# Scan of a Mamba-2 layer: the state's output moves into the chunk's own PSUM accumulation, with C times the decay made on VectorE

## The chip, the cores and the metric

The kernel runs on one core of one Trainium2 chip. The metric is the device time of one execution in microseconds, the median of several runs. All data are float32; large projections are made of three products of rounded halves (a high and a low part in fp32r), the scan's own products are plain float32.

## The reference, cut to what matters

The model is a trunk of two layers over 1024 positions of width 1024: a Mamba-2 layer, then shared keys and values, a stick-breaking attention layer, and a final norm. The change touches the Mamba-2 scan alone. Its step over chunks of 128 positions, for 4 groups of 8 heads (head width 64, state width 128):

```python
def step(state, inp):
    xc, ac, bc, cc = inp
    acum = jnp.cumsum(ac, axis=1)
    seg = jnp.where(causal, acum[:, :, None] - acum[:, None, :], -jnp.inf)
    scores = jnp.einsum('btgn,bsgn->btsg', cc, bc)[..., None] * jnp.exp(seg)
    y_diag = jnp.einsum('btsgh,bsghp->btghp', scores, xc)
    y_off = jnp.einsum('btgn,bghpn->btghp', cc, state) * jnp.exp(acum)[..., None]
    w_end = jnp.exp(acum[:, -1:] - acum)
    new_state = (state * jnp.exp(acum[:, -1])[..., None, None]
                 + jnp.einsum('bsgn,bsghp->bghpn', bc, xc * w_end[..., None]))
    return new_state, y_diag + y_off
```

After the scan come `y + d_skip * x`, the gate `y * silu(z)`, an RMS norm over each group's 512 channels, and the output projection. What the change rewrites is `y_diag + y_off`: exp(acum) may be multiplied onto C times the state, or onto C before the product.

## The kernel before, in words

**Stages.** First come the conditioning, the input projection and the causal convolution (to about 315 us of the span), then the scan (about 315 to 650 us), then the rest of the output projection, the shared keys and values, the attention and the final norm. The scan's inputs wait in DRAM: `xs_d` (convolved x, B, C), `ac_d` (acum per head), `ea_d` (exp(acum) per head).

**Units and chunks.** The scan works through 8 units: the 4 groups over the first half of the sequence, then the 4 groups over the second half. A unit has 4 chunks of 128 positions; the chunk index `c` runs from 0 to 7 in a group, and at c = 0 the state is empty. "The fourth unit" below is the last group over the first half (`st_2315` is its state); the fifth follows it.

**Names of one chunk.** `lm` (128x8x128) is acum broadcast to all partitions by a DMA (L509), masked on GpSimd (L515), passed through 8 exponentials on ScalarE (L518), and multiplied by `pb`, the scores C·B, on VectorE (L539). `xd` is x times dt (VectorE, from the transposes in `px`). `yd` (L550) is the chunk's own product, 8 matmuls of 64 output rows, one for each head; two heads lie side by side in one 128-row tile. `yo` (L560) is the state times C, 4 matmuls of 128 rows. `eb` is exp(acum) broadcast by two DMAs (L514), one for each half of the partitions, in a single buffer; VectorE multiplies `yo` by it (L562) and adds `yd` (L573), which gives `y`. `ps` (L565) is the new state's contribution `bs`·`xw`, added to the decayed state `sd` (GpSimd, L555) into `st`; at c = 0 ScalarE copies `ps` to `st` instead (L567), and VectorE copies `yd` to `y` (L571).

**What else TensorE does there.** Between these it projects z for the next unit: 3 k-steps of `pz` (a k-step is three matmuls, L129 to L131, with weights `hz`, `lz` split from the load `rz`), then the transposes of the next chunk, 3 more k-steps, the chunk's own products, 2 more k-steps. Before the products of a unit's third chunk stands `rs` (L599), the norm's sum of squares of the unit before: `gate` has made `y` times silu(z) (GpSimd), four squares on ScalarE (L587, L590) and their sums on GpSimd (L591). The last unit has no z left to project; there matmuls of the output projection (`po`, weights `ho`, `lo`, inputs `yh`, `yl`) stand between the chunks. Those inputs are the stored, normed y, loaded again (`yr`, L662, three buffers) and split on ScalarE (`yh`, L663) and VectorE (`yl`, L664) during the scan.

**What sets the order.** TensorE's order in the scan is that of the code. The order on VectorE, ScalarE, GpSimd and on SyncE, whose one queue issues all these loads, is set by a scheduler. Each engine works through its list in order, so an instruction that waits holds up what is listed behind it.

Of the kernel before, what the change touches and what calls it, by code (L numbers as in the profile page):

```python
# [12 lines left out]
F32 = mybir.dt.float32  # L13
# [39 lines left out]
def tile_trunk(ctx, tc, xT, xN, c, vec, ada0, adar, wxbc, wwave, wdt, wz, wmo, wk, wv, wq, wqz, wso, out):  # L53
# [413 lines left out]
    with ExitStack() as es:  # L467
# [32 lines left out]
        def chunk_a(u, c):  # L500
# [9 lines left out]
                        .rearrange("p (h t) -> p h t", t=P))  # L510
            eb = pq.tile([P, 4, P], F32, tag="eb", name="eb" + n, bufs=1)
            ev = ea_d[r0:r0 + 8, :].rearrange("(j a) t -> a j t", a=2)
            for a in range(2):
                Y.dma_start(out=eb[64 * a:64 * a + 64], in_=ev[a].partition_broadcast(64))  # L514
            Q.affine_select(out=lm, in_=lm, pattern=[[0, HPG], [1, P]], compare_op=ALU.is_ge,  # L515
                            fill=-1e30, base=0, channel_multiplier=-1)
            for h in range(HPG):
                e = S.activation(lm[:, h, :], lm[:, h, :], AF.Exp, bias=nac[:, c, h0_ + h:h0_ + h + 1])  # L518
                if g == 0 and c < 3:
                    tc.keep_in_program_order(e)  # L520
            px = ppt.tile([P, 512], F32, tag="px", name="px" + n)
            for j in range(4):
# [9 lines left out]
            if c < NC_ - 1:  # L532
                xw = py.tile([P, HPG, 64], F32, tag="xw", name="xw" + n)
                V.tensor_tensor(out=xw, in0=px3, op=ALU.mult,
                                in1=wdv[:, c, hsl].unsqueeze(2).to_broadcast([P, HPG, 64]))
                sp["xw"] = xw.rearrange("p h k -> p (h k)")
                sp["bs"] = py.tile([P, P], F32, tag="bs", name="bs" + n)
                S.copy(sp["bs"], pb[:, 0:P])
            V.tensor_tensor(out=lm, in0=pb[:, P:2 * P].unsqueeze(1).to_broadcast(sh3), in1=lm, op=ALU.mult)  # L539
            return sp, xd, lm, eb  # L540

        def chunk_b(u, c, sp, xd, lm, eb):
            g = u["g"]
            n = f"{g}_{c}"
            hsl = slice(HPG * g, HPG * g + HPG)
            cs = slice((c % CPH) * P, (c % CPH + 1) * P)
            ysl = u["y"][:, :, cs]
            yd = ppt.tile([P, 4, P], F32, tag="yd", name="yd" + n)
            for h in range(HPG):
                E.matmul(yd[64 * (h % 2):64 * (h % 2) + 64, h // 2, :], xd[:, h, :], lm[:, h, :],  # L550
                         start=True, stop=True)
            if 0 < c < NC_ - 1:

                sd = py.tile([P, HPG, 64], F32, tag="sd", name="sd" + n, bufs=1)
                Q.tensor_tensor(out=sd, in0=st[g].rearrange("p (h k) -> p h k", k=64), op=ALU.mult,  # L555
                                in1=eev[:, c, hsl].unsqueeze(2).to_broadcast([P, HPG, 64]))
            if c > 0:
                yo = ppt.tile([P, 4, P], F32, tag="yo", name="yo" + n)
                for j in range(4):
                    E.matmul(yo[:, j, :], st[g][:, j * P:(j + 1) * P], u["ct"][:, cs], start=True,  # L560
                             stop=True)
                V.tensor_tensor(out=eb, in0=yo, in1=eb, op=ALU.mult)  # L562
            if c < NC_ - 1:
                ps = ppt.tile([P, 512], F32, tag="ps", name="ps" + n)
                E.matmul(ps, sp["bs"], sp["xw"], start=True, stop=True)  # L565
                if c == 0:
                    S.copy(st[g], ps)  # L567
                else:
                    V.tensor_tensor(out=st[g], in0=ps, in1=sd.rearrange("p h k -> p (h k)"), op=ALU.add)
            if c == 0:  # L570
                V.tensor_copy(ysl, yd)  # L571
            else:
                V.tensor_tensor(out=ysl, in0=yd, in1=eb, op=ALU.add)  # L573

# [537 lines left out]
```

## Time and profile before

| | us |
|---|---|
| median of 3 runs | 1459.53 |
| lowest, highest | 1458.59, 1461.04 |
| the profiled execution's own time | 1462.46 |
| its span | 1460.8 |
| TensorE busy in the span | 1430.3 |
| VectorE, ScalarE, GpSimd busy | 962.0, 736.2, 516.5 |

The profile is one execution. A window row gives each engine's busy time in a stretch, TensorE's granted clock (1.00 is full speed) and the mean busy share of the 16 DMA engines. A timeline row gives start and length in us, and in brackets the idle time just before it with what ended it. The program counts a float32 matmul twice in the timeline (x16 for 8 matmuls). Where a `L` number stands, it is the line of the kernel.

### The profile page before, as it was taken

What the parts mean: (1) busy time and instruction counts of PE and PEld (TensorE: products, weight loads), DVE (VectorE), ACT (ScalarE), POOL (GpSimd) and SP (SyncE); (2) the same over time, 40 slices, a digit from 0 to 9 for tenths busy, and PEclk for the clock granted to TensorE, in tenths of its full rate; (3) what the DMA queues carried; (4) which work ended last, traced back from release to release, by engine and by line L of the source; (5) the groups of instructions that cost most, each with busy time, mean ns of one, the idle gap of its engine ahead of it and who ended that gap; (6) DMA issues with size and microseconds to landing.
All of it is one profiled execution on the core that took longest, in us unless ns stands there. A gap on an engine that the chain in (4) does not pass through costs nothing.

```text
span 1460.8 us, 20961 instructions
## 1 busy us (share of the span) xinstructions
PE 1430.3 (98%) x7772; PEld 1125.7 (77%) x7772; DVE 962.0 (66%) x1211; ACT 736.2 (50%) x1236; POOL 516.5 (35%) x601
## 2 busy tenths in 40 slices
PE   7998999999999999999999999999999999999997
PEld 4777888887777777778888888887777777777797
DVE  5699975455788887975733627516666666667674
ACT  6654533246666666733532424335555555556452
POOL 0021220002555555531011000027666666667531
PEclk9999999999999999999999999999999999999999
DMA  9358875233577766667433546460222122212253
GB/s 368 129 202 318 295 285 182 101 107 132 183 236 220 234 217 217 195 201 266 151 123 128 182 144 227 159 211 31 80 69 70 59 73 63 68 58 81 92 183 116
DMA packets 105446, 235.76 MB, mean 161 GB/s; under 512 B 9344, under 2 KB 40832, under 8 KB 103296
## 3 DMA queue, kind: packets, MB, share of 16 engines
q1 hardware_dynamic: 105344, 234.42, 47.8%
q8 instruction: 61, 1.00, 0.3%
q14 instruction: 41, 0.34, 0.1%
HBM read 188.51 MB, written 45.88 MB: 160 GB/s over the span
## 4 chain that ended last, share of the span: by engine, by line
PE 90%; DVE 5%; ACT 2%; issue 1%; DMA 1%; POOL 0%; SPq 0%; DVEq 0%; ACTq 0%; POOLq 0%
PE av L891 5%; PE pr L129 5%; PE pr L130 5%; PE pr L131 5%; PE sc L838 4%; PE at L870 4%; PE pz L129 4%; PE pz L131 4%; PE pz L130 4%; PE po L131 4%; PE po L130 4%; PE po L129 4%; PE pq L129 2%; PE pqz L129 2%; PE yd L550 2%; PE pq L131 2%
## 5 line engine op out<-in xcount | busy, mean ns | idle before, releaser
L861 POOL TENSOR_TENSOR be<-be,kp 128x1024 f32<-128x1024 f32 (+2 forms) x96 | 163.3, 1702 | 82.6 <-DVE kp L855 73.6
L841 ACT ACTIVATE kp<-sc 128x1024 f32<-128x1024 f32 (+2 forms) x96 | 75.5, 813 | 149.2 <-PE sc L838 111.3
L855 DVE TENSOR_TENSOR_SCAN kp<-kp,pone 128x128 f32<-128x128 f32 (+3 forms) x128 | 96.7, 803 | 63.8 <-POOL kp L848 63.8
L129 PE MATMUL pr<-h0h,hx 128*128 128x512 f32 x336 | 131.7, 392 | 3.8 <-DVE cv L353 3.8
L131 PE MATMUL pr<-h0h,lx 128*128 128x512 f32 x336 | 131.5, 391 | 0.0
L130 PE MATMUL pr<-h0l,hx 128*128 128x512 f32 x336 | 131.5, 391 | 0.0
L129 PE MATMUL pz<-h0h,hz 128*128 128x512 f32 x256 | 113.0, 441 | 0.0
L130 PE MATMUL po<-yl,ho 128*128 128x512 f32 x256 | 100.9, 394 | 0.6 <-DVE yl L664 0.6
L131 PE MATMUL po<-yh,lo 128*128 128x512 f32 x256 | 100.0, 391 | 1.3 <-DVE lo L124 1.3
L131 PE MATMUL pz<-h0h,lz 128*128 128x512 f32 x256 | 100.4, 392 | 0.0
L130 PE MATMUL pz<-h0l,hz 128*128 128x512 f32 x256 | 100.0, 391 | 0.0
L129 PE MATMUL po<-yh,ho 128*128 128x512 f32 x256 | 100.0, 391 | 0.0
L366 POOL TENSOR_TENSOR ar<-ar,crow 128x1024 f32<-128x1024 f32 x12 | 31.1, 2596 | 182.4 <-DMA ar<-adar 163.0
L518 ACT ACTIVATE lm<-lm,nac 128x128 f32<-128x128 f32 x256 | 78.9, 390 | 31.8 <-POOL lm L515 31.8
L855 DVE TENSOR_TENSOR_SCAN kp<-kp,ab,pone 128x512 f32<-128x512 f32 x64 | 78.3, 1265 | 24.7 <-ACT kp L841 14.2
L124 POOL TENSOR_TENSOR lq<-rq,hq 128x256 fp32r<-128x256 f32 x32 | 22.5, 738 | 177.8 <-ACT hq L123 177.8
L515 POOL TENSOR_SCALAR_AFFINE_SELECT lm<-lm 128x1024 f32<-128x1024 f32 x32 | 42.1, 1316 | 118.3 <-DMA lm<-ac_d 108.9
L555 POOL TENSOR_TENSOR sd<-st,eev 128x512 f32<-128x512 f32 x24 | 37.5, 1561 | 126.1 <-ACT st L567 114.2
L353 DVE SCALAR_TENSOR_TENSOR cv<-pr,vt,cv 128x1023 f32<-128x1023 f32 (+2 forms) x63 | 80.2, 1276 | 0.9
L129 PEld LDWEIGHTS pr<-h0h,hx 128*128 128x128 f32 x336 | 63.5, 189 | 17.4 <-issue 4.2
L123 ACT CAST ho<-ro 128x1024 fp32r<-128x1024 f32 x32 | 33.6, 1052 | 84.5 <-PE po L130 74.3
L870 PEld LDWEIGHTS at<-ident,be 128*128 128x128 f32 x576 | 67.2, 140 | 10.6 <-DVE aT L880 0.9
(258 smaller groups left out, 3886.7 us busy)
## 6 DMA issues: line engine op xcount, KB each, us to landing
ar<-adar SPq DMA_DIRECT2D x48, 512.0 KB, 5.3
lm<-ac_d SPq DMA_DIRECT2D x32, 512.0 KB, 5.0
rz<-wz SPq DMA_DIRECT2D x32, 512.0 KB, 3.8
ro<-wmo SPq DMA_DIRECT2D x32, 512.0 KB, 3.7
xs_d<-sv SPq DMA_DIRECT2D x24, 512.0 KB, 4.1
rx<-wxbc SPq DMA_DIRECT2D x21, 512.0 KB, 4.6
a<-ada SPq DMA_DIRECT2D x8, 1024.0 KB, 10.1
xg<-xs_d SPq DMA_DIRECT2D x8, 1024.0 KB, 6.1
```

Of the source, the lines that this page charges most:

```text
L129: E.matmul(ps, wh, xh, start=first, stop=False)
L130: E.matmul(ps, wh, xl, start=False, stop=False)
L131: E.matmul(ps, wl, xh, start=False, stop=last)
L353: V.scalar_tensor_tensor(out=ac[:, i:], in0=ps[:, :T - i], scalar=vv("cw", m * 4 + 3 - i), in1=ac[:, i:], op0=ALU.mult, op1=ALU.add)
L515: Q.affine_select(out=lm, in_=lm, pattern=[[0, HPG], [1, P]], compare_op=ALU.is_ge, fill=-1e30, base=0, channel_multiplier=-1)
L518: e = S.activation(lm[:, h, :], lm[:, h, :], AF.Exp, bias=nac[:, c, h0_ + h:h0_ + h + 1])
L838: E.matmul(ps[:, a, o:o + w], q[hsl[a], x, i * P:(i + 1) * P], kd[hsl[a], y, HT * c:HT * c + w], start=b == 0, stop=b == 2)
L841: S.activation(kp[:, :, ok:ok + w], ps[:, :, o:o + w], AF.Sigmoid, scale=-0.125)
L855: V.tensor_tensor_scan(out=ka, data0=ka, data1=pone.to_broadcast([P, w]), initial=1.0 if top else above[p, i][:, a, 0:1], op0=ALU.mult, op ...
L861: Q.tensor_tensor(out=be[:, :, o:o + w], in0=be[:, :, o:o + w], in1=kp[:, :, ok + 1:ok + w + 1], op=ALU.mult)
L870: E.transpose(ps[:, j, :], be[:, a, j * P:(j + 1) * P], ident)
L891: E.matmul(ps[hsl[a], cs], vd[:, j, hsl[a]], at[j // 4][:, a, j % 4, cs], start=j == 0, stop=j == nj - 1)
```

## The change

- `eb` becomes a tile of 128x8x128 with two buffers, the shape of `lm`: exp(acum) of 8 heads, broadcast to all 128 partitions by one DMA of 512 KB. It is loaded for c > 0 alone.
- VectorE multiplies it by C (`ct`), one instruction of 128x1024, both inputs in SBUF. It does not need the state, so it stands in `chunk_a`, a chunk ahead.
- TensorE: `yo` goes. For each pair of heads two matmuls of `xd`·`lm` start the accumulation in `yd`, and two of `st`·`eb` end it, all of 64 rows.
- ScalarE copies `yd` to `y` in every chunk; VectorE's product, addition and copy (L562, L573, L571) go.
- The PSUM bank of `yo` goes to `px`, which gets two. `xw` has one buffer instead of two. GpSimd's `sd` stands ahead of `yd` in the code.

```diff
-            eb = pq.tile([P, 4, P], F32, tag="eb", name="eb" + n, bufs=1)
-            ev = ea_d[r0:r0 + 8, :].rearrange("(j a) t -> a j t", a=2)
-            for a in range(2):
-                Y.dma_start(out=eb[64 * a:64 * a + 64], in_=ev[a].partition_broadcast(64))
+            eb = None
+            if c > 0:
+                eb = pq.tile(sh3, F32, tag="eb", name="eb" + n)
+                Y.dma_start(out=eb, in_=ea_d[r0:r0 + 8, :].rearrange("h t -> (h t)").partition_broadcast(P)
+                            .rearrange("p (h t) -> p h t", t=P))
...
-            px = ppt.tile([P, 512], F32, tag="px", name="px" + n)
+            px = ppt.tile([P, 512], F32, tag="px", name="px" + n, bufs=2)
...
-                xw = py.tile([P, HPG, 64], F32, tag="xw", name="xw" + n)
+                xw = py.tile([P, HPG, 64], F32, tag="xw", name="xw" + n, bufs=1)
...
             V.tensor_tensor(out=lm, in0=pb[:, P:2 * P].unsqueeze(1).to_broadcast(sh3), in1=lm, op=ALU.mult)
+            if c > 0:
+                V.tensor_tensor(out=eb, in0=ct[:, cs].unsqueeze(1).to_broadcast(sh3), in1=eb, op=ALU.mult)
...
-            yd = ppt.tile([P, 4, P], F32, tag="yd", name="yd" + n)
-            for h in range(HPG):
-                E.matmul(yd[64 * (h % 2):64 * (h % 2) + 64, h // 2, :], xd[:, h, :], lm[:, h, :],
-                         start=True, stop=True)
...
-            if c > 0:
-                yo = ppt.tile([P, 4, P], F32, tag="yo", name="yo" + n)
-                for j in range(4):
-                    E.matmul(yo[:, j, :], st[g][:, j * P:(j + 1) * P], u["ct"][:, cs], start=True,
-                             stop=True)
-                V.tensor_tensor(out=eb, in0=yo, in1=eb, op=ALU.mult)
+
+            yd = ppt.tile([P, 4, P], F32, tag="yd", name="yd" + n)
+            for j in range(4):
+                o = [yd[64 * a:64 * a + 64, j, :] for a in range(2)]
+                for a in range(2):
+                    E.matmul(o[a], xd[:, 2 * j + a, :], lm[:, 2 * j + a, :], start=True, stop=c == 0)
+                for a in range(2 if c > 0 else 0):
+                    h = 2 * j + a
+                    E.matmul(o[a], st[g][:, h * 64:h * 64 + 64], eb[:, h, :], start=False, stop=True)
...
-            if c == 0:
-                V.tensor_copy(ysl, yd)
-            else:
-                V.tensor_tensor(out=ysl, in0=yd, in1=eb, op=ALU.add)
+            S.copy(ysl, yd)
```

The scheduler's lists change with it, at three places that matter below. In a row of such a list a name's last number marks the instance, and "waits DMAHW2_49" names the queue or engine whose semaphore is waited for.

SyncE's queue in the fourth unit, before: the two loads of the unused `eb` of the fifth unit's chunk 0, then those of chunk 1 into the same buffer, then `lm`, the 1 MB load `xg` and the last `yr` of these.

```order
L662 DMA yr_0_5378<-ys_d_0_78 128x512 [waits DMAHW4_49,DMAHW2_49,DVE_49]
L514 DMA eb_0_3501<-ea_d 64x4x128 [waits DVE_49]
L514 DMA eb_0_3501<-ea_d 64x4x128 [waits DMAHW3_49]
L118 DMA rz_1_3_3857<-wz 128x1024 [waits DVE_49]
L514 DMA eb_1_3614<-ea_d 64x4x128 [waits DMAHW5_49,DMAHW3_49,DMAHW2_49]
L514 DMA eb_1_3614<-ea_d 64x4x128 [waits DMAHW6_49]
L509 DMA lm_3_3772<-ac_d 128x1024 [waits DMAHW7_49,PE_49]
L489 DMA xg_1_3588<-xs_d_70 128x4x512 [waits DMAHW0_49,DVE_49]
L662 DMA yr_0_5382<-ys_d_0_78 128x512 [waits DMAHW1_49,DVE_49]
```

The same stretch of SyncE's queue, now:

```order
L661 DMA yr_0_5410<-ys_d_0_76 128x512 [waits DMAHW7_49,DVE_49]
L509 DMA lm_2_3694<-ac_d 128x1024 [waits DMAHW0_49,PE_49]
L514 DMA eb_2_3696<-ea_d 128x1024 [waits DMAHW1_49,PE_49]
L661 DMA yr_0_5414<-ys_d_0_78 128x512 [waits DMAHW2_49,DVE_49]
L661 DMA yr_0_5418<-ys_d_0_78 128x512 [waits DMAHW3_49,DVE_49]
L489 DMA xg_1_3594<-xs_d_70 128x4x512 [waits DMAHW4_49,DVE_49]
L661 DMA yr_0_5422<-ys_d_0_78 128x512 [waits DMAHW7_49,DMAHW5_49,DVE_49]
L118 DMA rz_1_3_3867<-wz 128x1024 [waits DMAHW6_49,DVE_49]
L509 DMA lm_3_3780<-ac_d 128x1024 [waits PE_49]
```

No load of a chunk 0's `eb` stands there any more, `eb` waits for TensorE's last use of its buffer instead of VectorE's and a landing, and `yr` stands ahead of `xg`.

ScalarE at the start of the fifth unit, before: the state's copy first, the squares among the `yh` casts, the fourth square behind the last `yh` and 8 exponentials.

```order
L567 COPY st_2315<-ps_0_3661 128x512
L587 ACTIVATE sq_0_3569<-y_0_2847 128x512
L123 CAST hz_1_2_3758<-rz_1_2_3756 128x1024
L663 CAST yh_0_5332<-yr_0_5374 128x512
L590 ACTIVATE sq_0_1_3575<-y_0_2847 128x512
L590 ACTIVATE sq_0_2_3580<-y_0_2847 128x512
L663 CAST yh_0_5334<-yr_0_5378 128x512
L482 COPY sz_1_3594<-pz_1_0_3602 128x512
L538 COPY bs_2_3716<-pb_2_3709 128x128
L663 CAST yh_0_5336<-yr_0_5382 128x512
L518 ACTIVATE lm_3_3772<-lm_3_3772,nac 128x128 x8
L590 ACTIVATE sq_0_3_3585<-y_0_2847 128x512
```

The same place of ScalarE's list, now:

```order
L539 COPY bs_1_3645<-pb_1_3638 128x128
L586 ACTIVATE sq_0_3575<-y_0_2847 128x512
L589 ACTIVATE sq_0_1_3581<-y_0_2847 128x512
L589 ACTIVATE sq_0_2_3586<-y_0_2847 128x512
L572 COPY y_0_3224<-yd_0_3658 128x4x128
L569 COPY st_2315<-ps_0_3667 128x512
L662 CAST yh_0_5376<-yr_0_5418 128x512
L123 CAST hz_1_2_3766<-rz_1_2_3764 128x1024
L482 COPY sz_1_3600<-pz_1_0_3608 128x512
L589 ACTIVATE sq_0_3_3591<-y_0_2847 128x512
```

Three squares and the copy of `yd` stand ahead of the state's copy; the fourth square stands ahead of the exponentials and of all `yh` casts but one.

TensorE in the last unit, before: the products of chunk 6 in one piece, between matmuls of the output projection.

```order
L131 MATMUL po_0_5487<-yh_0_5336,lo_0_0_5491 128x512
L550 MATMUL yd_6_5229<-lm_6_5133,xd_6_5157 64x128 x8
L560 MATMUL yo_6_5240<-ct_1_4712,st_2315 128x128 x4
L565 MATMUL ps_6_5246<-xw_6_5159,bs_6_5161 128x512
L129 MATMUL po_0_5487<-yh_0_5338,ho_0_1_5520 128x512
```

The same chunk in TensorE's list, now:

```order
L130 MATMUL po_0_5465<-yl_0_5395,ho_0_1_5498 128x512
L561 MATMUL yd_6_5271<-lm_6_5171,xd_6_5194 64x128 x2
L131 MATMUL po_0_5465<-yh_0_5394,lo_0_1_5499 128x512
L129 MATMUL po_0_5465<-yh_0_5396,ho_0_1_5498 128x512
L130 MATMUL po_0_5465<-yl_0_5397,ho_0_1_5498 128x512
L131 MATMUL po_0_5465<-yh_0_5396,lo_0_1_5499 128x512
L130 MATMUL po_0_5531<-yl_0_5369,ho_0_0_5534 128x512
L131 MATMUL po_0_5531<-yh_0_5368,lo_0_0_5535 128x512
L129 MATMUL po_0_5531<-yh_0_5370,ho_0_0_5534 128x512
L130 MATMUL po_0_5531<-yl_0_5371,ho_0_0_5534 128x512
L564 MATMUL yd_6_5271<-eb_6_5173,st_2315 64x128 x2
L561 MATMUL yd_6_5271<-lm_6_5171,xd_6_5194 64x128 x2
```

The first two matmuls of 64 rows stand alone, eight of the output projection follow, and the other fourteen come after them; chunk 7 is split in the same way.

## Rows read from the trace of the kernel before

**Rows 1.** The page: span, and the chain that ended last, by engine.

```profile
span 1460.8 us, 20961 instructions
...
PE 90%; DVE 5%; ACT 2%; issue 1%; DMA 1%; POOL 0%; SPq 0%; DVEq 0%; ACTq 0%; POOLq 0%
```

**Rows 2.** Windows: PE, PEld, DVE, ACT, POOL busy (count), granted clock, DMA share, GB/s.

```profile
315.00:650.00 335.00, 330.03 (x1941) 258.16 (x1940) 270.93 (x320) 211.65 (x448) 151.47 (x104) 0.99 0.61 198
450.00:460.00 10.00, 9.62 (x57) 7.12 (x57) 10.00 (x11) 9.97 (x18) 8.89 (x6) 1.00 0.71 187
470.00:480.00 10.00, 8.01 (x39) 6.01 (x40) 6.17 (x9) 6.88 (x17) 4.42 (x4) 0.83 0.48 157
600.00:620.00 20.00, 18.18 (x98) 13.81 (x97) 20.00 (x22) 15.95 (x32) 12.80 (x9) 1.00 0.61 196
```

**Rows 3.** TensorE's waits in the scan: total us, times, longest.

```profile
PE rs L599 <- POOL sq L591: 2.8, 1, 2.8
PE po L131 <- DVE lo L124: 1.3, 1, 1.3
PE po L130 <- DVE yl L664: 0.6, 2, 0.3
```

**Rows 4.** TensorE's timeline, fifth unit: products of chunks 0 and 1.

```profile
451.07 1.09 PE L550 MATMUL yd<-lm,xd 128*64 128x128 f32 x16
...
452.66 0.80 PE L129 MATMUL pz<-h0h,hz 128*128 128x512 f32 x1
...
459.89 1.09 PE L550 MATMUL yd<-lm,xd 128*64 128x128 f32 x16 [0.38 <-DVE lm L539]
460.91 1.16 PE L560 MATMUL yo<-ct,st 128*128 128x128 f32 x8
461.91 1.02 PE L565 MATMUL ps<-xw,bs 128*128 128x512 f32 x2
462.37 0.80 PE L129 MATMUL pz<-h0h,hz 128*128 128x512 f32 x1
```

**Rows 5.** TensorE's timeline, fifth unit: the norm's sum and chunk 2.

```profile
471.99 1.12 PE L599 MATMUL rs<-sq,ones 128*128 128x512 f32 x2 [2.77 <-POOL sq L591]
473.05 1.97 PE L550 MATMUL yd<-lm,xd 128*64 128x128 f32 x16
474.95 1.89 PE L560 MATMUL yo<-ct,st 128*128 128x128 f32 x8
476.67 1.02 PE L565 MATMUL ps<-xw,bs 128*128 128x512 f32 x2
```

**Rows 6.** ScalarE's timeline in the fifth unit.

```profile
457.22 0.58 ACT L567 COPY st<-ps 128x512 f32<-128x512 f32 x1
...
467.04 0.62 ACT L663 CAST yh<-yr 128x512 fp32r<-128x512 f32 x1 [5.05 <-DMA yr<-ys_d]
467.57 2.45 ACT L518 ACTIVATE lm<-lm,nac 128x128 f32<-128x128 f32 x8
469.92 0.61 ACT L590 ACTIVATE sq<-y 128x512 f32<-128x512 f32 x1
```

**Rows 7.** SyncE's queue: its wait in 449 to 472 us, and an issue.

```profile
SPq L514 <- DMA eb<-ea_d: 3.8, 1, 3.8
...
458.64 0.32 SPq L662 DMA_DIRECT2D yr<-ys_d  x1
```

**Rows 8.** Landing of `yr` (425 to 475 us).

```profile
DMA to landing us min/median/max: 3.5/4.5/8.4
```

**Rows 9.** One instruction, ns min/median/max: `lm` and `lz` on VectorE.

```profile
L539 DVE TENSOR_TENSOR lm<-pb,lm x32: 1203/1211/1225, 329.8 to 627.1; 128x1024 f32<-128x1024 f32 x32
...
L124 DVE TENSOR_TENSOR lz<-rz,hz x31: 1208/1520/2304, 314.5 to 583.3; 128x1024 fp32r<-128x1024 f32 x31
```

**Rows 10.** Groups by form: busy us, mean ns | idle before, releaser.

```profile
L562 DVE TENSOR_TENSOR eb<-yo,eb 128x512 f32<-128x512 f32 x28 | 19.2, 684 | 7.9 <-PE yo L560 4.3 <-DMA eb<-ea_d 3.3
...
L573 DVE TENSOR_TENSOR y<-yd,eb 128x512 f32<-128x512 f32 x28 | 19.2, 684 | 0.4
...
L482 ACT COPY sz<-pz 128x512 f32<-128x512 f32 x32 | 18.5, 578 | 0.0
```

## The prediction

> **What bounds the kernel now.** I read first the chain that ended last: 90% of it is TensorE [rows 1]. Then the scan's window: TensorE is busy in 330.03 of 335.00 us, so at most 4.97 us of waiting can be won there, at a granted clock of 0.99; VectorE has 270.93, ScalarE 211.65, the DMA engines a share of 0.61 [rows 2]. Outside the scan the change touches only a few loads and products that fall into slack of the convolution. So the questions are: does TensorE's own work in the scan change, which of the four waits go, and which new one comes. The list of TensorE's waits names them: 2.8 us before the norm's sum `rs`, 1.3 and 0.6 before `po` in the last unit [rows 3], and 0.38 before `yd`, in the bracket of its row [rows 4]. Their sum, 5.1, is the window's idle time.
>
> The large wait has a tail. After it `yd` takes from 473.05 to 474.95, 1.90 us, where it took 1.02 (459.89 to 460.91) two chunks earlier, and `yo` 1.72 (474.95 to 476.67) instead of 1.00 [rows 4, 5]; the window 470 to 480 has a granted clock of 0.83 [rows 2]. TensorE had idled 2.77 us just before. The stretch ran at half clock, 1.2 instead of 2.4 GHz, and cost 0.88 + 0.72 = 1.60 us more.
>
> Where that wait comes from I followed backwards. `rs` waits for GpSimd's sum, that for ScalarE's fourth square, which started at 469.92, behind 8 exponentials (2.45 us), behind a `yh` cast at 467.04 that had waited 5.05 us for its load [rows 6]. The load `yr` was issued at 458.64 and landed 8.4 us later (the median is 4.5) [rows 7, 8]. It was late at SyncE: the queue stood 3.8 us, at the load of chunk 1's `eb`, until the unused `eb` of chunk 0 had landed in the same buffer [rows 7]; behind it came `lm`, the 1 MB `xg`, then `yr`.
>
> **The change part by part.**
>
> *TensorE.* A chunk with state lasts from `yd` at 459.89 to the next `pz` at 462.37, 2.48 us; one without state from 451.07 to 452.66, 1.59 [rows 4]. So the 8 records of `yo` cost 0.89, 0.11 each. The 16 of `yd` take 1.02; at half clock 1.90. With a part f that does not scale, 2 × (1.02 − f) + f = 1.90, so f = 0.14 and the matmuls are 0.88, 0.055 each: two of 64 rows take the time of one of 128, side by side. The 16 new records of `st`·`eb` in the same alternation cost 0.88 for 0.89 removed: −0.01 × 28 chunks = −0.3. Bounds: without overlap 16 × 0.11 = 1.78, +0.89 × 28 = +24.9; if f is a start-up that adjoining work hides, nothing below −0.3. I take −0.3, as the new matmuls have the shape, the width and the pairing of the row. In the last unit the list now splits chunks 6 and 7, two matmuls and then fourteen; that makes two more groups of 64 rows, each with an f of 0.14 in and, I assume, as much out: 2 × 0.28, about +0.5 (0 to +0.6).
>
> That f is the row's. The Trainium skill, "TensorEngine Tiling (Array Packing)", section "Key Properties", says that a change of the tiling mode drains the engine; it gives no price, so by it alone the split is a loss of unknown size, which the 0.14 of this trace agrees with.
>
> *VectorE.* Out go 28 products and 28 additions of 0.684 each, and 4 copies of about that [rows 10]: 41.0 us. In come 28 products of 128x1024 with two SBUF inputs. The trace has no such instruction; nearest are `lm`, same size with one input in PSUM, 1.21 us at any time, and `lz`, same size with both in SBUF, 1.21 to 2.30, median 1.52 [rows 9]. So 28 × (1.21 to 2.30) = 34 to 64; I take `lz`'s median, 42.6, since both inputs match. Net +1.6 of 270.9, ends −7 and +23. The 64 us left idle hide the mean case, but not in places: VectorE is busy 20.00 of 20.00 us between 600 and 620, in the last unit, and 10.00 of 10 between 450 and 460 [rows 2]. In return the product stands a chunk ahead and no longer between TensorE's product and `y`. `xw` in one buffer makes its product wait for `ps` of the chunk before; behind `lm` in VectorE's list it has most of a 9 us chunk to spare: nothing, or 0.4 if it delays the next product.
>
> *ScalarE.* In come 32 copies of 128x512 out of PSUM; the copy of `pz` takes 0.578 [rows 10]: +18.5 on 211.65, which TensorE's 330 us covers. It does not cover one place, the start of the fifth unit: 9.97 of 10 us busy [rows 2]. There the state's copy ended at 457.22 + 0.58 = 457.80 [rows 6], and TensorE reads it from chunk 1 on: before at `yo`, 460.91, now inside `yd`, which without its 0.38 wait starts at 459.51 [rows 4]. The margin was 3.1 and is 1.7. In front of that copy now stand two more copies of `yd` (1.16) and three squares (0.61 each, 1.83), 3.0 in all: 1.3 late. Against that, ScalarE's chain there starts with a `yh` cast that waits for a `yr` load; a load 1 us earlier gives 1 us back, one with the longest landing instead of the median takes 8.4 − 4.5 = 3.9 [rows 8]. I take a new wait of 1.0, near the row's own reckoning; bounds 0 and 3.9.
>
> *Loads.* 64 loads of 128 KB become 28 of 512 KB: 8.4 MB become 14.7, +6.3 on the 66 MB that 198 GB/s move in 335 us [rows 2]. The share goes from 0.61 to 0.67, not the bound; transfers may land later, which the 3.9 above holds. SyncE's 3.8 us stop goes: the load behind it is no longer made, and the new `eb` waits for TensorE's `yd` of chunks long done.
>
> *The old waits.* With `yr` ahead of `xg` and the fourth square ahead of the exponentials and the later casts, the sum for `rs` should be ready some 4 us earlier than 471.99, more than the 2.77: −2.77, and −1.60 for the clock. The 0.38 goes with the reordering of VectorE's list. The last unit's 1.3 + 0.6 I leave: they end with splits of weights and inputs that VectorE makes, and VectorE is full there. What is late next is the state's copy above.
>
> **Sum.** −2.77 − 1.60 − 0.38 = −4.75; +1.0 new wait; −0.3 + 0.5 on TensorE: −3.55. The profiled execution took 1462.46 (span 1460.8 [rows 1]) and would take 1458.9; it lies 2.9 above the median of 1459.53, so the forecast for the median is 1456.0. Its own range: the new wait from 0 to 2.5, the split from 0 to 0.6, and spread between runs: 1453.5 to 1458.6. A difference under 0.2%, 2.9 us, can't be told from none here.
>
> **Rivals.**
>
> *B, the wait comes back.* ScalarE at the start of the fifth unit becomes what the SyncE stop was. For it: 9.97 of 10 busy and 3.0 us put in front of a copy that TensorE needs. Against it: the chain can start earlier with its load. Price: a wait of 1.3 plus half of the 3.9 is 3.2, as long as the one that was followed by half clock, so +1.6 again: −4.75 + 3.2 + 1.6 + 0.2 = +0.25, 1459.8. No change.
>
> *C, all waits go.* If the new product a chunk ahead relieves VectorE in the last unit, 1.9 more goes and the new wait does not come: −4.75 − 1.9 − 0.3 + 0.5 = −6.45, 1453.1. Against it: VectorE's sum there does not fall.
>
> *D, slower: VectorE's product pays for two SBUF inputs.* `lz` reaches 2.30, `lm`, of the same size with one, never passes 1.23 [rows 9]; GpSimd works 8.89 of 10 and 12.80 of 20 us just in those windows [rows 2]. At 2.30 a product and sum of 1.37 is replaced by 0.93 more. Where VectorE is full TensorE sees it: three products in the last unit's full window, +2.8, and one at each of the six other gates, whose sums VectorE starts, +5.6. The waits that I strike then stay, because the squares come later: 1459.5 + 8.4 = 1467.9. It decides from a mean of about 1.8 us upward, where 9 × 0.43 uses up the 3.55. Against it: the median of `lz` is 1.52.
>
> The Trainium skill, "SBUF — State Buffer", section "Who interferes with whom", states that a VectorE instruction with two SBUF inputs contends with a GpSimd instruction that reads SBUF, and one with a single SBUF input does not. The trace agrees in that `lz` spreads from 1.21 to 2.30 us and `lm` does not. By this rule the product that is added is of the exposed kind and both that go are not, which is rival D.
>
> *E, the pairs do not overlap.* If matmuls that end an accumulation cannot run side by side as those that start it: +24.9, 1480.9. Against it: the pairing is that of the row; the trace has no accumulating pair.
>
> **How the numbers follow.** Forecast 0.42, B 0.30, C 0.10, D 0.13, E 0.05. Range: below, C's case less 2, 1451.0; above, half of D, 1464.0; E, the upper part of D and C's tail stay out, about 0.2. Faster by over 0.2% means under 1456.6: of the forecast 0.26, of B 0.03, C 0.10: 0.39. Slower means above 1462.4: D 0.13, E 0.05 and 0.04 of B: 0.22. Within: 0.16 + 0.23 = 0.39.
>
> **What would show it.** Right: no wait before `rs` in the fifth unit and a full granted clock in it; no SyncE wait at `eb`; a block of 2.4 to 2.5 us from `yd` to the next `pz`; copies of about 0.58 on ScalarE; `eb` products with a mean near 1.5. A wait of TensorE for ScalarE's copy of `ps` or `yd` at chunk 1 of the fifth unit shows the new term, with its size. Wrong: blocks of 3.3 us (E), products over 1.8 with VectorE ending TensorE's waits (D), or a wait in another unit where ScalarE or a load is late, which I have not priced.

## The result, and the profile after

The changed kernel is slower. Its first four executions gave 1476.84 us in the median (1473.34 to 1480.69) against 1459.06 for the kernel before, a ratio of 1.0123 [1.0086, 1.0160]; four more gave 1475.93 and 1.0114 [1.0101, 1.0127]. The forecast was 1456.0. The profiled execution took 1473.34 us. Of the first four executions two took 1473.3 and 1473.5 us, at a mean granted clock of 0.995, and two 1480.2 and 1480.7, at 0.992 and 0.990; what parts the pairs stays open.

The page after answers to [rows 1]: the chain that ended last is TensorE's to 81% instead of 90%; VectorE and the DMAs now hold 8% and 3% of it.

```profile
span 1471.6 us, 21305 instructions
...
PE 81%; DVE 8%; DMA 3%; ACT 2%; POOL 2%; issue 2%; SPq 0%; DVEq 0%; POOLq 0%; ACTq 0%
```

The scan's window, as the first row of [rows 2]: VectorE is no busier than before (267.67 for 270.93), ScalarE a little more. In a full stretch of 335 us TensorE idles 15.4 instead of 5.0.

```profile
315.00:650.00 335.00, 319.63 (x2110) 246.60 (x2109) 267.67 (x279) 223.03 (x473) 158.62 (x102) 0.99 0.63 214
```

TensorE's waits in the scan, as [rows 3]. Their sum is 15.3 us, 10.2 more than before; the two profiled executions differ by 10.9. So the loss is waiting. 9.0 us of it are put down to VectorE (2.3 before), 4.5 to ScalarE (none before) and 1.8 to GpSimd (2.8 before).

```profile
PE pz L131 <- DVE lz L124: 4.1, 6, 1.8
PE ps L567 <- DVE st L571: 3.6, 3, 1.6
PE yd L561 <- ACT st L569: 3.0, 1, 3.0
PE rs L598 <- POOL sq L590: 1.8, 1, 1.8
PE po L129 <- ACT yh L662: 1.5, 1, 1.5
PE po L130 <- DVE yl L663: 1.3, 1, 1.3
```

The `rs` of this list is in the last unit. In the fifth unit `rs` no longer waits, as forecast.

TensorE's own work is what was forecast. A chunk with state, as the second half of [rows 4]: each row is one input of a pair of heads, the rows start some 0.22 us apart, and from `yd` to the next `pz` it is 512.17 to 514.63, 2.46 us for 2.48 before.

```profile
512.17 0.44 PE L561 MATMUL yd<-lm,xd 128*64 128x128 f32 x4
512.44 0.39 PE L564 MATMUL yd<-eb,st 128*64 128x128 f32 x4
...
514.07 1.12 PE L567 MATMUL ps<-xw,bs 128*128 128x512 f32 x2
514.63 0.80 PE L129 MATMUL pz<-h0h,hz 128*128 128x512 f32 x1
```

The new instructions, grouped by form as [rows 10]: the product takes 1.44 us in the mean (1.52 was taken), the copy 0.574 (0.578). New is the idle time on the right: VectorE stood 25.9 us before the product, waiting for its load. Of VectorE's waits in 315 to 650 us the same wait is 21.4; for the `eb` of the kernel before it was 3.3 [rows 10].

```profile
L542 DVE TENSOR_TENSOR eb<-ct,eb 128x1024 f32<-128x1024 f32 x28 | 40.3, 1439 | 25.9 <-DMA eb<-ea_d 25.9
...
L572 ACT COPY y<-yd 128x512 f32<-128x512 f32 x32 | 18.4, 574 | 8.2 <-PE yd L564 8.1
```

Why the load is late shows in the landing times of the two kernels (loads, KB each, median us from issue to landing):

```profile
eb<-ea_d SPq DMA_DIRECT2D x64, 128.0 KB, 3.3
...
eb<-ea_d SPq DMA_DIRECT2D x28, 512.0 KB, 5.9
```

VectorE reads `eb` about as long after the issue as before: in the median 8.3 us now, and 7.7 from the later of the two loads before. But the load takes 5.9 us to land instead of 3.3, so that in the median 1.3 us are left between landing and use where 4.4 were; 13 of the 28 products start as their load lands. An estimate from the 11 waits in 315 to 650 us (0.6 to 3.5 us each): if each load had landed 2.6 us sooner, about 2 of the 21.4 us would be left. No run tried smaller loads.

How this reaches TensorE can be read in three places. First, VectorE's timeline in a later unit. At 540.36 it is done with `st` and waits 2.27 us for the decay's load; the split `lz` stands behind the product.

```profile
539.68 0.68 DVE L571 TENSOR_TENSOR st<-ps,sd 128x512 f32<-128x512 f32 x1
542.63 1.25 DVE L542 TENSOR_TENSOR eb<-ct,eb 128x1024 f32<-128x1024 f32 x1 [2.27 <-DMA eb<-ea_d]
543.80 2.10 DVE L124 TENSOR_TENSOR lz<-rz,hz 128x1024 fp32r<-128x1024 f32 x1
```

TensorE's timeline: it needed that `lz` 0.58 us earlier than it was there.

```profile
545.96 0.50 PE L131 MATMUL pz<-h0h,lz 128*128 128x512 f32 x1 [0.58 <-DVE lz L124]
```

SyncE's timeline: the next weight load `rz` goes out the moment `lz` has freed its buffer, and the next decay's load 0.9 us behind it. VectorE's next product starts at 553.07, after 3.09 us of waiting.

```profile
545.93 0.33 SPq L118 DMA_DIRECT2D rz<-wz  x1
546.32 0.42 SPq L509 DMA_DIRECT2D lm<-ac_d  x1
546.83 0.38 SPq L514 DMA_DIRECT2D eb<-ea_d  x1
```

Second, a unit's end in the first half. The gate's four sums (L582) can start as soon as ScalarE has copied `yd`, and stand in VectorE's list ahead of the state's sum `st`, which frees the bank of `ps`.

```profile
448.20 2.73 DVE L582 SCALAR_TENSOR_TENSOR y<-xg,vt,y 128x512 f32<-128x512 f32 x4
450.85 0.68 DVE L535 TENSOR_TENSOR xw<-px,wdv 128x512 f32<-128x512 f32 x1
451.45 0.67 DVE L571 TENSOR_TENSOR st<-ps,sd 128x512 f32<-128x512 f32 x1
```

TensorE's next `ps` waits for it, and ten microseconds later comes the third place, which the prediction had named: `yd` waits for the state's copy.

```profile
452.18 1.13 PE L567 MATMUL ps<-xw,bs 128*128 128x512 f32 x2 [1.55 <-DVE st L571]
...
462.59 0.44 PE L561 MATMUL yd<-lm,xd 128*64 128x128 f32 x4 [3.02 <-ACT st L569]
```

ScalarE's timeline there, as [rows 6]: a `yh` cast waited 7.42 us for its `yr`, and the whole list behind it came late, the state's copy to 462.02 from 457.22.

```profile
450.37 0.62 ACT L662 CAST yh<-yr 128x512 fp32r<-128x512 f32 x1 [7.42 <-DMA yr<-ys_d]
...
462.02 0.58 ACT L569 COPY st<-ps 128x512 f32<-128x512 f32 x1
```

### The profile page after: what moved, and what is told of

Same layout as the page of the kernel before. It is cut to its first block, busy times and chain, and to the rows that moved or that the text cites. A ratio compares the mean times of both kernels' runs of the same rounds, so it can differ in the third digit from the quotient of the medians.

```text
span 1471.6 us, 21305 instructions
## 1 busy us (share of the span) xinstructions
PE 1430.2 (97%) x7996; PEld 1122.6 (76%) x7996; DVE 964.0 (66%) x1179; ACT 752.1 (51%) x1268; POOL 529.7 (36%) x601
## 4 chain that ended last, share of the span: by engine, by line
PE 81%; DVE 8%; DMA 3%; ACT 2%; POOL 2%; issue 2%; SPq 0%; DVEq 0%; POOLq 0%; ACTq 0%
PE av L890 5%; PE pr L129 4%; PE pr L131 4%; PE pr L130 4%; PE sc L837 4%; PE at L869 4%; PE po L131 4%; PE po L129 4%; PE po L130 4%; PE pz L131 2%; PE pq L129 2%; PE pz L129 2%; PE pz L130 2%; PE pqz L129 2%; PE pq L131 2%
## 5 line engine op out<-in xcount | busy, mean ns | idle before, releaser
L554 POOL TENSOR_TENSOR sd<-st,eev 128x512 f32<-128x512 f32 x24 | 33.7, 1406 | 167.8 <-ACT st L569 118.3
L869 PEld LDWEIGHTS at<-ident,be 128*128 128x128 f32 x576 | 67.2, 140 | 10.4 <-DVE aT L879 0.7
L869 PE MATMUL at<-ident,be 128*128 128x128 f32 x576 | 74.7, 272 | 0.5 <-DVE aT L879 0.5
## 6 DMA issues: line engine op xcount, KB each, us to landing
a<-ada SPq DMA_DIRECT2D x8, 1024.0 KB, 10.2
```

Source lines behind the costliest of these rows:

```text
L869: E.transpose(ps[:, j, :], be[:, a, j * P:(j + 1) * P], ident)
```

## The experiments

All ratios are to the kernel before, on the same chip, with a 95% interval. "Product" is VectorE's C times decay, "load" that of the decay. The runs were made on several chips, on which the kernel before has medians of 1459.2 to 1460.2 us; differences between medians of different chips carry that much more.

| run | what | median us | ratio |
|---|---|---|---|
| e1 | changed kernel again | 1475.93 | 1.0114 [1.0101, 1.0127] |
| e2 | before, no unused load | 1458.60 | 0.9996 [0.9988, 1.0005] |
| e3 | no product | 1463.11 | 1.0025 [1.0015, 1.0035] |
| e4 | copies on VectorE | 1471.14 | 1.0085 [1.0065, 1.0105] |
| e5 | `st` ahead of the gate's sums | 1472.79 | 1.0093 [1.0077, 1.0108] |
| e6 | load on ScalarE's queue | 1476.70 | 1.0111 [1.0096, 1.0126] |
| e7 | product pinned late | 1636.21 | 1.1217 [1.1200, 1.1233] |
| e8 | product on GpSimd | 1480.88 | 1.0147 [1.0133, 1.0161] |
| e9 | before again, one execution | 1460.89 | |
| e10 | product, no load | 1466.41 | 1.0048 [1.0036, 1.0060] |
| e11 | no product, no load | 1462.14 | 1.0012 [1.0000, 1.0023] |
| e12 | C from PSUM | 1479.23 | 1.0135 [1.0122, 1.0149] |
| e13 | control: two `yr` buffers | 1484.83 | 1.0176 [1.0163, 1.0189] |
| e14 | e13, third decay buffer | 1478.74 | 1.0137 [1.0120, 1.0154] |
| e15 | e13, load not awaited | 1490.77 | 1.0204 [1.0189, 1.0219] |
| e16 | e11, copies on VectorE | 1462.91 | 1.0022 [1.0013, 1.0032] |
| e17 | e10, `st` first | 1466.44 | 1.0043 [1.0030, 1.0056] |
| e18 | e11, `st` first | 1461.21 | 1.0011 [1.0001, 1.0021] |

**e1, no edit.** 

> The changed kernel once more, for its spread: its four executions so far gave 1473.3, 1473.5, 1480.2 and 1480.7 us. If the 7 us between the two pairs belong to the execution, both values come again here; if they belong to the chip or the day, one value comes, within about 3 us. TensorE's waits in the scan should again sum to about 15 us when the time is near 1473.

One value came, 1475.0 to 1477.7; the 1480 of two early executions did not. TensorE's waits sum to 15.7 us, close to the 15.3, but are named otherwise: 13.2 are put down to VectorE and 2.2 to ScalarE. In these two executions the sum agrees and the single places do not.

```profile
PE pz L131 <- DVE lz L124: 5.1, 5, 1.8
PE ps L567 <- DVE st L571: 4.9, 3, 1.9
PE po L129 <- ACT yh L662: 2.2, 1, 2.2
PE yd L561 <- DVE lm L540: 2.0, 2, 1.4
```

The 3.0 for ScalarE's copy is not in the list, but the copy is as late as in the first profile. At the same place `yd` waits 1.44 us, put down to VectorE's `lm`, which ended 0.2 us after ScalarE's copy of the state:

```profile
464.06 0.44 PE L561 MATMUL yd<-lm,xd 128*64 128x128 f32 x4 [1.44 <-DVE lm L540]
...
463.15 0.58 ACT L569 COPY st<-ps 128x512 f32<-128x512 f32 x1
```

**e2 and e9, the wait that the prediction struck.**

```diff
-            for a in range(2):
+            for a in range(2 if c > 0 else 0):
                 Y.dma_start(out=eb[64 * a:64 * a + 64], in_=ev[a].partition_broadcast(64))
```

> The kernel before, with one edit: the decay of chunk 0, which nothing uses, is not loaded. Theory of the prediction: SyncE's 3.8 us stop at that buffer made the load yr late, and through it rs waited 2.77 us and the next stretch ran at half clock (1.60): both go, 1459 to about 1455. Rival: the load yr is late because 1.5 MB go ahead of it in the queue, and it lands as late as before: rs still waits about 2.8, 1459.

> The kernel before, once more with a profile. The prediction took its profiled execution (1462.46, the highest of those then known) for the rule and struck a wait of 2.8 before rs with 1.6 of half clock. If that wait belongs to the kernel it stands here again, 2 to 3 us in the fifth unit. If it belonged to that one execution, rs waits under 0.5 here, and the execution is nearer 1459.

In e2 `rs` does not wait at all. Yet the time does not move clear of the noise: 0.9996. e9 says why. In another execution of the unchanged kernel `rs` waits 0.5 us:

```profile
PE po L131 <- DVE lo L124: 1.3, 1, 1.3
PE rs L599 <- POOL sq L591: 0.5, 1, 0.5
```

The 2.77 us were those of one execution, which lay 2.9 above the median. Nor do the two runs bear out the prediction's chain from SyncE's stop to that wait. The first three rows are e9's, the last two e2's:

```profile
SPq L514 <- DMA eb<-ea_d: 3.2, 1, 3.2
458.48 0.32 SPq L662 DMA_DIRECT2D yr<-ys_d  x1
464.56 0.62 ACT L663 CAST yh<-yr 128x512 fp32r<-128x512 f32 x1 [2.82 <-DMA yr<-ys_d]
...
SPq L489 <- DVE y L583: 5.0, 1, 5.0
457.94 0.32 SPq L662 DMA_DIRECT2D yr<-ys_d  x1
```

e9 has the stop too, 3.2 us long, and its `yr` went out at 458.48, where it was 458.64 in the first profile. But it had landed after 6.1 us instead of 8.4. In e2 the stop is gone, and `yr` still went out only 0.7 us sooner, because SyncE now waited 5.0 us at `xg`. So the two waits, 2.77 and 0.5, differ by the 2.3 us by which that one load landed later. Why it did stays open.

**e3, e10 and e11, product and load.** e3 feeds the loaded decay to TensorE without C; e10 multiplies C by C and loads nothing; e11 feeds C itself.

```diff
-                V.tensor_tensor(out=eb, in0=ct[...], in1=eb, op=ALU.mult)   # e3: left out
...
-                Y.dma_start(out=eb, in_=ea_d[...])                          # e10: left out
-                V.tensor_tensor(out=eb, in0=ct[...], in1=eb, op=ALU.mult)
+                V.tensor_tensor(out=eb, in0=ct[...], in1=ct[...], op=ALU.mult)
```

> The changed kernel without VectorE's product of C and the decay: TensorE multiplies the state by the loaded decay itself, so the factor C is left out. Theory 1, VectorE's list (the products, which wait for their load, stand in front of the splits lz and yl and of the state's sum st): TensorE's waits for lz (4.1 us in 6 places) go, those of ps for st (3.6) shrink, and the yr loads come earlier, so that the 3.0 for ScalarE shrinks too; about 8 us or more under the changed kernel. Theory 2, ScalarE's copies of yd: the 3.0 in the fifth unit and the 1.8 before rs stay, at most 4 us come back. Theory 3, the larger loads land too late: the wait moves to TensorE, which then waits for the load of the decay itself, and the time stays near 1473.

> The changed kernel whose product multiplies C by C: same instruction, both inputs in SBUF, 28 of them, but the decay is not loaded and not applied. Theory 1b, the product's time on VectorE: as slow as the changed kernel, 1473 to 1477, with waits for lz, st and yl of 10 to 15 us in all. Theory 1c, the product's wait for its load (21 us of VectorE's idle time in the changed kernel): near the kernel without the product, 1461 to 1466.

> The changed kernel without the decay: no load of it and no product, TensorE multiplies the state by C itself; the factor exp(acum) is left out. Without the product alone 1463.1 was measured. If what is left over the kernel before (3.4 us) is the larger loads, this comes to 1459 or under; if it is ScalarE's copies of yd, it stays at 1462 to 1464.

Without the product 12.8 us come back (1475.9 to 1463.1). With the product but without its load 9.5 come back. In e10 the product takes as long as ever, but waits for nothing, and TensorE's waits for `lz`, 4.1 and 5.1 before, are gone from the list; those for `st` stay:

```profile
L540 DVE TENSOR_TENSOR eb<-ct 128x1024 f32<-128x1024 f32 x28 | 39.1, 1401 | 0.2 <-DMA ct<-xs_d 0.2
...
PE ps L565 <- DVE st L569: 4.1, 3, 1.7
PE yd L562 <- DVE st L569: 1.9, 1, 1.9
```

So most of the loss is the product's wait for its load, not its length. e11 against e3 says what the load costs where no product waits for it: 1.0 us, within the intervals of nothing. So the four kernels stand at 1462.1 with neither, 1463.1 with the load, 1466.4 with the product and 1475.9 with both: what costs most needs both. A caveat: between the profiles of e10 and of the changed kernel about 140 of VectorE's 1179 instructions, 60 of ScalarE's 1268 and 75 of GpSimd's 601 stand in other places of their lists.

**e13, e14 and e15, the same question with the lists held.** e13 makes room, with a buffer less for `yr` and a small table in another pool (not in the cut below); e14 adds the third decay buffer, after which the lists of TensorE, ScalarE and GpSimd are the same.

```diff
-    pyr = pool(esy, "pyr", bufs=3)
+    pyr = pool(esy, "pyr", bufs=2)
...
-                eb = pq.tile(sh3, F32, tag="eb", name="eb" + n)
+                eb = pq.tile(sh3, F32, tag="eb", name="eb" + n, bufs=3)   # e14 alone
```

> Control: the changed kernel with two buffers for yr instead of three and one small table moved to another pool, which makes room for the next two runs. Expected near the changed kernel, 1473 to 1479; a later yr may cost 1 to 3 us.

> The control with a third buffer for the decay; the lists of TensorE, ScalarE and GpSimd are the same, 26 rows of VectorE's and SyncE's differ, since the loads can stand earlier. Theory 1c, the product's wait for its load: VectorE's idle time before the product falls from over 15 us to under 8, the waits for lz shrink, 3 to 8 us faster than the control. Theory 1b, the product's own time and place: less than 1 us.

> The control with the decay loaded as before into a buffer that nothing reads, while the product multiplies C by C: the traffic and the place in SyncE's queue stay, the wait goes, the decay is not applied. If the wait is what costs, 7 to 10 us under the control, about 1467; if the traffic or the queue costs, near the control.

The control missed its bounds, at 9 us over the changed kernel: the third `yr` buffer is worth far more than the 1 to 3 us expected (the moved table was not tried alone). Against it e14 is 6.1 us faster. The product's row in e13 and in e14: a longer product and a shorter wait, and the time goes with the wait. ScalarE's wait for `yr` falls too, from 30.9 to 24.5 us, so that the pair does not single out the product's wait.

```profile
L543 DVE TENSOR_TENSOR eb<-ct,eb 128x1024 f32<-128x1024 f32 x28 | 43.4, 1549 | 28.2 <-DMA eb<-ea_d 28.2
```

```profile
L543 DVE TENSOR_TENSOR eb<-ct,eb 128x1024 f32<-128x1024 f32 x28 | 45.2, 1613 | 21.3 <-DMA eb<-ea_d 21.2
```

The wait did not fall under 8, as expected of an earlier load. The buffer held little of it: SyncE stood at the decay's loads for 2.1 us in all even in e13. e15 does not answer its question. Its loads went into one buffer, so each waited for the landing of the one ahead, and SyncE stood 93.1 us at them:

```profile
SPq L516 <- DMA el<-ea_d: 93.1, 27, 5.8
```

It shows only what such a stop costs.

**e5, e17 and e18, the place of `st`.** The state's sum of a unit's last chunk and the gate's sums are kept in the order of the code.

```diff
+                    if c % CPH == CPH - 1:
+                        tc.keep_in_program_order(e)     # e = the state's sum st
...
+                tc.keep_in_program_order(e)             # e = the gate's sums y<-xg,vt,y
```

> The changed kernel with VectorE's list pinned at the four unit ends of the first half: the sum st that frees the bank of ps stands ahead of the gate's four sums, as in the kernel before, instead of behind them. If the wait of ps for st (3.6 and 4.9 us in the two profiles) is a matter of that place in the list alone, it goes, and the time falls by 3 to 5 us, to about 1471. Rival: VectorE is full there and something else listed behind becomes as late (the gate's sums, then rs): the wait changes its name and the time stays within 1 us.

> The kernel whose product multiplies C by C without a load (1466.4; the decay is left out), with the state's sum pinned ahead of the gate's sums. Its waits of ps for st were 4.1 us. If wait and place are all of the loss, it comes to 1462 or 1463, level with the kernels that have no product; if the product's own time on VectorE costs 4 us, the waits move and it stays at 1465 to 1467.

> The kernel without any decay (1462.1), with the state's sum pinned ahead of the gate's sums. Its waits were 2.1 for rs, 1.5 for lz, 1.5 for st. If the place of st is the rest of the loss, 1460 to 1461, level with the kernel before; if the waits move to rs or lz, 1462 or more.

In e5 TensorE no longer waits for `st`, and 3.1 us come back; but `lz` now takes 9.0 us in 4 waits, one of 6.1. In e17 the same pin brings nothing at all:

```profile
PE pz L131 <- DVE lz L124: 4.4, 4, 2.1
PE yd L562 <- DVE st L569: 1.9, 1, 1.9
```

The 4.1 us moved from `st` to `lz`. So in e17 the place of `st` decides which instruction is late, not whether one is. e17 against e18, which has no product, prices the 40 us of product that nothing holds up: 1466.4 to 1461.2, 5.2 us.

**e4 and e16, the copies.**

```diff
-            S.copy(ysl, yd)
+            V.tensor_copy(ysl, yd)
```

> The changed kernel with the 32 copies of yd on VectorE instead of ScalarE. Theory 1, VectorE's list is what is full: 32 copies of about 0.68 us more on it, the waits for lz and st grow, 2 to 10 us slower than the changed kernel. Theory 2, ScalarE at the start of the fifth unit: TensorE's wait of 3.0 for the copied state goes or falls under 1, the waits for lz stay, 3 to 5 us faster than the changed kernel.

> The kernel without any decay (1462.1), with the copies of yd on VectorE instead of ScalarE. If ScalarE's copies are the rest of the loss over the kernel before, 1459 to 1460; if not, 1462 or more.

e4 made VectorE busier by 16.5 us in 315 to 650 us (284.21 for 267.67) and became 4.8 us faster. That refutes theory 1 in the form of a full VectorE. Theory 2 isn't shown by it either: the waits for `lz`, which it let stand, fall to 1.1, and in place of the 3.0 `yd` waits 4.3 us for `lm`. Much changes at once in e4: the product's wait falls from 21.4 to 10.6 us, ScalarE is 14 us less busy, and in the fourth unit `st` is back ahead of the gate's sums. Which of these wins the 4.8 us stays open. In e16, without product and load, the engine of the copy makes no difference.

**e6, e8 and e12, the load or the product elsewhere.**

```diff
-                Y.dma_start(out=eb, in_=ea_d[...])
+                S.dma_start(out=eb, in_=ea_d[...])                          # e6
...
-                V.tensor_tensor(out=eb, in0=ct[...], in1=eb, op=ALU.mult)
+                Q.tensor_tensor(out=eb, in0=ct[...], in1=eb, op=ALU.mult)   # e8
...
+                S.copy(pb[:, 2 * P:3 * P], ct[:, cs])                       # e12
+                V.tensor_tensor(out=eb, in0=pb[:, 2 * P:3 * P]..., in1=eb, op=ALU.mult)
```

> The changed kernel with the decay's 512 KB loads issued from ScalarE's queue instead of SyncE's; VectorE's list is almost the same. Theory 1a, a loop through SyncE's one queue (the decay's load stands behind a weight load rz that waits for lz, and lz stands behind the product that waits for the decay's load): the waits for lz (4.1 and 5.1 us) go, 1471 or less. Rival 1b, the product's own time on VectorE makes lz late: they stay, about 1475. If ScalarE is held up by issuing the loads, its own waits (yh, st) grow and it gets slower.

> The changed kernel with the product of C and the decay on GpSimd instead of VectorE, 28 of them. VectorE then has what it has without the product (the run without it came to 1463.1). Theory 1 (the product in VectorE's list): 1461 to 1466, if GpSimd, busy 158 of 335 us, takes 28 more of about 2 us without being late. Rival: GpSimd becomes late with the masks of lm, the decayed state sd or the squares' sums, and contends with VectorE's two-input instructions: TensorE waits for POOL, 1470 or more.

> The changed kernel with C copied by ScalarE into a free part of the bank of the scores (28 copies of 128x128, about 0.25 us each), so that VectorE's product has one input in PSUM and one in SBUF, as lm has. If two SBUF inputs beside GpSimd make it dear, its mean falls from 1.44 to about 1.21 (lm: never over 1.23), VectorE wins 6.5 us, and the time falls by 2 to 5 us, less what ScalarE loses. If the size of the product counts alone, the mean stays above 1.4 and the time stays at 1474 to 1478.

e6 is inconclusive. VectorE's wait for the load fell from 21.4 to 8.3 us, but it then waited 20.6 for `bs` and 10.4 for the norm's root, both ScalarE's (12.9 and 2.4 in the changed kernel), and `lz` still cost 4.8. So a loop through SyncE's queue alone is not what makes `lz` late. In e8 the product takes 2.56 us on GpSimd and TensorE's waits grow to 20 us. In e12 no product is over 1.226 us, and the kernel is 3 us slower. The product now waits for ScalarE's copy, as long as it had waited for its load; where the 3 us come from was not looked into:

```profile
L543 DVE TENSOR_TENSOR eb<-pb,eb 128x1024 f32<-128x1024 f32 x28 | 34.2, 1222 | 24.1 <-ACT pb L542 24.1
```

Over the whole of each profile, the kernels whose product waits 21 to 28 us, for a DMA or for ScalarE (the changed one, e5, e12, e13, e14), lie at 1472.8 to 1484.8; e4, where it waits 15, at 1471.1; e10 and e17, where it waits 1 us or less, at 1466.4. e6 is the exception, with 13 us and 1476.7 (e7, e8 and e15, which change more, are left aside).

**e7, the product just ahead of its use.**

```diff
+                tc.keep_in_program_order(e)             # e = lz, the product, st, the gate's sums
```

> The changed kernel with VectorE's list pinned in two ways: the state's sum ahead of the gate's sums, and the product of C and the decay behind the split lz and the product lm, just ahead of its use. Theory 1, what stands behind the product in VectorE's list pays: waits for lz and st go, about 8 us faster than the changed kernel, 1467, unless TensorE then waits for the product itself. Rival, VectorE's total work decides, not its order: the waits for lz go and waits for the product or for yl of the same size come, 1474 to 1476.

The product's line also moves from `chunk_a` to just ahead of `yd`. Pinning so much took the lead out of VectorE's list: `xw` waits for `ps`, the next `lz` stands behind it, and TensorE waits 54.6 us for `lz` and 43.6 for the product. The expected gain was not tested by it.

No version of the changed kernel beats the kernel before. Even e11, which has neither product nor load, does not.

## Why the prediction was wrong

**The gain was not there to be had.** The prediction took −4.75 us, of them 4.37 from the wait of `rs` and its stretch at half clock. But the wait belonged to the profiled execution (1462.46); in e9 it is 0.5, with a stop of SyncE of 3.2, and e2, without that stop, is not faster clear of the noise. The sign stood in the text: that execution "lies 2.9 above the median". The gain was taken off a median that hardly contains it.

**The step that failed is the product's wait for its load, which had no term.** "In return the product stands a chunk ahead" and "The 64 us left idle hide the mean case" priced its length, 42.6 us for 41.0, which was right (40.3). Nothing priced its wait. The load goes out earlier than before, in the median 15.8 us ahead of its chunk's block on TensorE instead of 5.8, but VectorE also wants it a chunk earlier, and at 512 KB it lands in 5.9 us instead of 3.3: 21.4 us of waiting for 3.3, in a list where `lz`, `yl` and `st` stand behind it. The prediction counted the larger loads in megabytes and in SyncE's stops; nothing in it sets their landing against the product's start. The sentence on the loads, "transfers may land later, which the 3.9 above holds", put that risk on `yr` alone. By e1, e10, e17 and e18, the loss of about 16 us (1475.9 against 1459.8) is some 9.5 for the load, of which about 1 comes without a product that waits (e1 less e10, e3 less e11), some 5 for the product once nothing awaits a load (e17 less e18), and 1 to 2 for the rest, whose cause stays open. The intervals leave each of these uncertain by 2 to 3 us.

**What had no term.** The order in which VectorE's list takes the gate's sums and `st` changed, perhaps because the copy by ScalarE makes `y` ready sooner; the rows of that list were not looked at for it. It names 3.6 to 4.9 us of the waits, though e17 shows that the pin alone does not win them.

**The new wait.** It came where it was forecast, with 3.02 us for a forecast of 1.0 and rival B's 3.2, through the late `yr`. In e1 ScalarE's copy is as late, and TensorE waits 1.44 us there.

**Rival D** forecast the right sign from 1.8 us per product upward. The product has 1.44, under the 1.8 from which it was to decide. Of its mechanism, a VectorE that is late by the length of its products, the 5.2 us of e17 less e18 can be seen, at a mean of 1.40; the larger part of the loss is the wait, which D does not hold. **Rival E** is refuted by the 2.46 us block, and no wait stands beside the split in the last unit; what the split itself costs was not measured. **Half clock** was taken as what follows a long wait; see below.

## What to carry to other kernels

Before a wait is counted as a gain, see whether the profiled execution is a typical one: take the spread of the runs, and a second profile if there is one. For an instruction that is moved earlier, ask when its inputs land and how much longer a larger load takes to land, not only how long the instruction takes: in a list that is worked through in order, its wait is paid by everything behind it. An engine that is 80% busy can be given more work and the kernel still get faster, as in e4; so the sum of busy time alone does not tell whether what another engine needs is late.

## What the runs showed of the hardware

**The clock.** The prediction had half clock follow a long wait. After the 3.02 us wait of the changed kernel it did not come; it came in the same execution around a wait of 1.77:

```profile
462.00:470.00 8.00, 7.41 (x58) 6.08 (x59) 7.89 (x8) 6.91 (x18) 6.51 (x5) 1.00 0.45 134
...
580.00:590.00 10.00, 8.23 (x54) 6.22 (x53) 7.69 (x7) 6.30 (x15) 5.91 (x5) 0.85 0.42 138
```

In e1 the same instruction waits 1.80 us in the same window, and the clock stays full:

```profile
580.00:590.00 10.00, 8.20 (x58) 6.02 (x57) 7.18 (x7) 6.57 (x15) 7.62 (x6) 1.00 0.41 159
```

In the first profile of the kernel before, the wait of 1.3 in the last unit left the clock at 1.00 (600 to 620 in [rows 2]). In e9 half clock stands around the same wait:

```profile
610.00:620.00 10.00, 8.65 (x38) 6.47 (x40) 8.62 (x10) 3.76 (x11) 6.67 (x5) 0.83 0.66 203
```

So each of the two profiles of the kernel before holds one such stretch in the scan, after different waits, and e2's, at 1.00 throughout, none. The 1.6 us do not go with one wait.

**Two inputs in SBUF.** The Trainium skill, "SBUF — State Buffer", section "Who interferes with whom", lets a VectorE instruction with two SBUF inputs contend with GpSimd's reads, and one with a single SBUF input not. The runs agree: 28 products with both inputs in SBUF take 1.21 to 2.30 us, 1.44 in the mean; with C in PSUM (e12) 1.207 to 1.226. In the changed kernel's trace the 14 products beside which GpSimd ran nothing take 1.21 to 1.23 us, and all ten over 1.4 ran beside its work; in e12 ten ran beside it, and none is longer for it.
